# Even-layer bursts with the sums of values behind the scores, and odd-layer dilated scores on 64 rows with zero columns

## The chip, the cores and the metric

The kernel runs on one core of one Trainium2 chip. A core has a tensor engine (PE, whose weight loads are listed as PEld), a vector engine (DVE), a scalar engine (ACT), GpSimd (POOL) and queues that issue DMAs (here nearly all on SyncE, SP). The metric is the device time of one execution in microseconds (us), as the median of several runs. The profile is that of one execution.

## The reference

Two layers of a hybrid encoder trunk on one sequence of 256 tokens of width 1024, all in float32. Layer 0 is even, layer 1 is odd. Cut to what matters here:

```python
for layer in range(2):
    xn = rms_norm(x, norm_mix[layer])
    x = x + (even_mixer if layer % 2 == 0 else odd_mixer)(xn, ...)
    x = x + sq_relu_mlp(rms_norm(x, norm_mlp[layer]), w1[layer], w2[layer])
return rms_norm(x, norm_final)

# even: 8 heads of neighbourhood attention (scores + bias, softmax, sum of values) and
#       8 heads of latent attention (a 64-wide and a turned 32-wide part), side by side,
#       then one output projection of width 1024
# odd:  16 heads; for each of 3 groups of keys (window, stride) = (128,1), (512,4), (2048,16)
#       scores are taken at those offsets alone; the three groups are joined in one softmax:
sc = einsum('bqhd,bqjhd->bhqj', q_blk, k_sel) * scale     # per group, masked where outside
out = softmax over the three groups' entries, times their values, summed; then @ w_o
```

With 256 tokens, group 1 pairs each token with those of the same remainder modulo 4, and group 2 with those of the same remainder modulo 16. The kernel's host code orders the tokens so that the 64 tokens of one remainder modulo 4, a "class", stand together; a tile of 128 tokens then holds two classes, and the scores of groups 1 and 2 are needed only inside a class, a 64 by 64 block. A mask does the rest.

## The kernel before, in words

Everything lives on chip but the weights, which stream in as 64 or so chunks of 1 MB by DMA on SP's queue into four buffers `raw`. Products in float32 are made of parts that the tensor engine takes at full rate: each operand is split into a high part (a cast on ACT, L178) and a low part (a subtraction on DVE, L179), and a product is three matmuls (`mm3`, L182 to L184) or two (`mm2`, L188 and L189). Each weight chunk is so split in four pieces: four ACT casts `whi` and four DVE subtractions `wlo`. These pieces are spread over the whole program and share the two engines with the softmaxes. Some small matmuls (transposes, sums of values, and the odd layer's group 1 and 2 scores) take plain float32 instead.

The phases follow each other: even mixer, MLP 0, odd mixer, MLP 1 with the final norm. A tile framework schedules the instructions of each engine from the order in which the code issues them, from priorities (`soon()` raises that of the copies and splits that empty PSUM) and from its own estimates; a semaphore wait keeps each dependency. PSUM has eight banks here: four under the tag `acc` and four under `w`, and each tag is handed round in turn, so that a new tile waits until the tile that had the bank four allocations earlier has been read.

**Even mixer.** `main` is a list of 32 steps of large products: 12 steps of query and key projection (`qk_steps`, 12 mm3 matmuls of 256 columns each), 8 steps of latent queries, keys and values (12, 6 or 3 matmuls), and 12 steps of output projection (`out_steps`, 12 matmuls each; step 20 is the first). Behind some of the steps stands a `burst(hp)`: it handles one pair of heads (`hp` 0 to 3 neighbourhood, 4 to 7 latent):

- `turn_pair(hp - 1)` transposes the probabilities of the pair before (16 transposes, L748, into two `w` banks, copied out at L752 by ACT or DVE as `pts`);
- `pair_scores` or `latent_scores` makes the scores of pair `hp` (12 matmuls at L203 or 24 at L701, into two `w` banks). Their two heads j = 0 and 1 use rows 0 to 63 and 64 to 127 of the array. The softmax follows on DVE and ACT: maxima (L731 or L705), exponentials (L734 or L708), reciprocals, then the scaling to `pp` (L736 and L737, or L713 and L715), which the transposes of the next burst read;
- `mix(a, b)` makes the sums of values of two pairs, 32 matmuls at L767 (two instructions each) into one bank, `acc` as long as the output projection's four accumulators `accs` aren't open (step 19), `w` after; it reads the `pts` of both pairs and is split to `oa` or `ob`, which the output projection reads.

In a burst with a `mix`, the `mix` comes first, ahead of the transposes and scores. After step 31 and `mix(6, 7)` follow the last products (`out_last`, which need both splits of that `mix`), then `hand_over`, which prepares the MLP's input `xT`.

**Odd mixer.** Eight units of two heads. A unit's projections run as large products (`qk_steps`, `value_steps`); after the sixth step of unit u + 1 stands the `burst` of unit u: transposes of the unit before (L936, 12), scores of group 0 (`two_heads`, L203, 12), 12 more transposes, and the scores of groups 1 and 2 (L914): 16 matmuls, each of a class's 64 queries by its 64 keys, two instructions each, for i (tile of tokens), g (group), c (class in the tile) and j (head). Queries of both groups are in `q12`, keys in `k12`, both written by one DVE addition after the rotary turn (L890).

**Final norm.** The last 128 rows are scaled in two column parts, 640 by DVE and 384 by ACT, and each part leaves in one DMA, the first on SP's queue, the second on ACT's (L473 to L476).

Of the kernel before, what the change touches and what calls it, by code (L numbers as in the profile page):

```python
# [16 lines left out]
F32 = mybir.dt.float32  # L17
F32R = mybir.dt.float32r
AF = mybir.ActivationFunctionType
ALU = mybir.AluOpType  # L20
# [3 lines left out]
P = 128  # L24
D = 1024
KT = D // P
T = 256
NT = T // P
# [18 lines left out]
def trunk(ctx, tc, a, out):  # L47
    nc = tc.nc
# [26 lines left out]
    def halves(z):  # L75

        return (z[:, 0, :], z[:, 1, :]) if len(z.shape) == 3 else (z[:, :, 0, :], z[:, :, 1, :])

    def bank(tag):
        return ps.tile([P, 512], F32, tag=tag, name=tag)  # L80
# [96 lines left out]
    def split(hi, lo, src, eng=None):  # L177
        a = nc.scalar.copy(hi, src).ins  # L178
        return a, (eng or nc.vector).tensor_tensor(lo, src, hi.bitcast(F32), op=ALU.subtract).ins  # L179
# [38 lines left out]
    def tok(t):  # L218
        return slice(t * P, (t + 1) * P)
# [41 lines left out]
    def inverse_columns(s):  # L261

        inv = columns(s)
        nc.vector.reciprocal(inv, inv)
        return inv
# [148 lines left out]
    def finish(mp, xT, s):  # L414

        HALF = [slice(0, 512), slice(512, D)]
        g = mp.tile([P, D], F32, name="gain")
        nc.sync.dma_start(g, a["norm_final"].partition_broadcast(P))
        xt = mp.tile([P, NT, D], F32, name="xt")
        tail = range(13, 16)  # L420

        def tokens_first(j):

            if j % 2 == 0 and j < 8:
                t, h = j // 4, j // 2 % 2
                pt = bank("w")
                for k in range(4):
                    nc.tensor.transpose(pt[:, k * P:(k + 1) * P], x[:, 4 * h + k, tok(t)], ident)
                nc.scalar.copy(xt[:, t, HALF[h]], pt)

        accs, hs, inv, w = mlp(mp, xT, lambda: inverse_columns(s), tail, make_down([15] * 3 + [tail[0] - 1]), tokens_first)
        jf = [(j, f) for j in w for f in range(2)]
        for j, f in jf:
            for h in range(2):
                mm_tokens(accs[h], hs, j, w[j], f, 0, h * 512, h * 512 + 512, False, (j, f) == (15, 1))

        def residual(t, cs, acc):
            nc.vector.scalar_tensor_tensor(xt[:, t, cs], acc, column(inv, t), xt[:, t, cs], ALU.mult, ALU.add)

        def square_sum(v, o):  # L440
            nc.scalar.activation(scratch([v.shape[-1]], "junk"), v, AF.Square, scale=D ** -0.5, accum_out=o)

        ss = work.tile([P, 4], F32, tag="ssf", name="ss")
        for h, cs in enumerate(HALF):
            residual(0, cs, accs[h])
            square_sum(xt[:, 0, cs], ss[:, h:h + 1])
        nc.vector.tensor_scalar(ss[:, 2:3], ss[:, 0:1], ss[:, 1:2], EPS, ALU.add, ALU.add)
        r = rsqrt(ss[:, 2:3], "x")
        for h, cs in enumerate(HALF):
            y = scratch([512], "y")  # L450
            nc.vector.scalar_tensor_tensor(y, xt[:, 0, cs], r, g[:, cs], ALU.mult, ALU.mult)
            nc.sync.dma_start(out[0:P, cs], y)


        ss = work.tile([P, 4], F32, tag="ssf", name="ss")
        xg = mp.tile([P, D], F32, name="xg")
        residual(1, HALF[1], accs[3])
        for i, (c0, c1) in enumerate(((0, 512), (512, 768), (768, D))):
            acc = bank("w") if i else accs[2]
            for n, (j, f) in enumerate(jf):  # L460
                mm_tokens(acc[:, 0:c1 - c0], hs, j, w[j], f, 1, c0, c1, i > 0 and n == 0, n == len(jf) - 1)
            v = xt[:, 1, c0:c1]
            residual(1, slice(c0, c1), acc[:, 0:c1 - c0])
            if i < 2:
                square_sum(v, ss[:, i:i + 1])
            else:
                nc.vector.tensor_scalar(ss[:, 2:3], ss[:, 0:1], ss[:, 1:2], EPS, ALU.add, ALU.add)
                nc.vector.tensor_tensor_reduce(out=scratch([c1 - c0], "junk"), in0=v, in1=v, op0=ALU.mult, op1=ALU.add,
                                               scale=1.0 / D, scalar=ss[:, 2:3], accum_out=ss[:, 3:4])
            nc.vector.tensor_tensor(xg[:, c0:c1], v, g[:, c0:c1], op=ALU.mult)  # L470
        r = rsqrt(ss[:, 3:4], "x")
        cs = slice(0, 640), slice(640, D)
        nc.vector.tensor_scalar(xg[:, cs[0]], xg[:, cs[0]], r, None, ALU.mult)  # L473
        nc.sync.dma_start(out[P:T, cs[0]], xg[:, cs[0]])
        nc.scalar.activation(xg[:, cs[1]], xg[:, cs[1]], AF.Copy, scale=r)
        nc.scalar.dma_start(out[P:T, cs[1]], xg[:, cs[1]])  # L476


    def even(ep):
# [291 lines left out]
                split(*halves(mixed[kind][:, hp:hp + n]), pvo[:, 0:n * T].rearrange("p (i n) -> p i n", i=n))  # L771

        def burst(hp, *mixes):
            if mixes:
                mix(*mixes)
            if hp > 0:
                turn_pair(hp - 1)
            if hp < 8:
                (pair_scores if hp < 4 else latent_scores)(hp)

        ug, kg = query_steps(), key_value_steps()
        first = qk_steps(0)
# [12 lines left out]
        main = [f for c in range(1, 4) for f in qk_steps(c)] + [kg[0], ug[0], ug[1], kg[1], kg[2], ug[2], kg[3], ug[3]]  # L795
        main += [f for k in range(6) for f in out_steps(accs, mixed, wo, k)]
        beside = {0: [turn_c[1]], 3: [turn_keys], 19: [lambda: accs.extend(open_accs())]}
        for at, *n in ((1, 0), (5, 1), (9, 2), (13, 3, 0, 1), (17, 4), (20, 5, 2, 3), (23, 6), (26, 7, 4, 5), (29, 8)):
            beside.setdefault(at, []).append(lambda n=n: burst(*n))
        beside.setdefault(31, []).append(lambda: mix(6, 7))  # L800
        for i, step in enumerate(main):
            step()
            run_all(beside.get(i, ()))
# [3 lines left out]
    def odd(op, xT, s):  # L807
# [5 lines left out]
            nc.sync.dma_start(dst, a[nm])  # L813
        mixed = [quarter_pair("oa"), quarter_pair("ob")]

        def unit_tiles(u):
            d = {}
            for n, shape, dt in (("q0", [P, 2, 2, T], F32R), ("q12", [P, 2, T], F32), ("k12", [P, 2, T], F32)):
                d[n] = op.tile(shape, dt, tag=n, name=n, bufs=2)
            return d  # L820

        values = {}
# [36 lines left out]
        def qk_steps(d):  # L859


            hold = {}

            def gemm(b, f, half):
                if f == 0 and half == 0:
                    hold["w"], hold["s"] = weight(), scratch([2, T], "qk")
                if half == 0:
                    hold["p"] = bank("acc")
                (wh, wl), s, pq = hold["w"], hold["s"], hold["p"]
                for k in range(4 * half, 4 * half + 4):  # L870
                    ws = slice((f * KT + k) * P, (f * KT + k + 1) * P)
                    mm2(pq, wh[:, ws], wl[:, ws], xT[:, k], k == 0, k == KT - 1)
                if half == 1:
                    with soon():
                        joined(s[:, f], pq)
                if f == 1 and half == 1:
                    rope(b, s)

            def rope(b, s):
                sw, r1 = scratch([2, T], "sw"), scratch([2, T], "r1")  # L880
                for r in range(0, P, 64):
                    nc.sync.dma_start(sw[r:r + 32], s[r + 32:r + 64])
                    nc.sync.dma_start(sw[r + 32:r + 64], s[r:r + 32])
                nc.vector.tensor_tensor(r1, s, cosT.unsqueeze(1).broadcast_to([P, 2, T]), op=ALU.mult)
                nc.vector.tensor_tensor(sw, sw, sinT.unsqueeze(1).broadcast_to([P, 2, T]), op=ALU.mult)
                if b == 0:
                    nc.vector.tensor_tensor(r1, r1, sw, op=ALU.add)
                    split(*halves(d["q0"]), r1)
                else:
                    nc.vector.tensor_tensor(d[("q12", "k12")[b - 1]], r1, sw, op=ALU.add)  # L890

            return [lambda v=(b, f, h): gemm(*v) for b in range(3) for f in range(2) for h in range(2)]

# [9 lines left out]
        def scores(u, d, between):  # L903

            ss = {(i, j): bank("w") for i in range(NT) for j in range(2)}
# [3 lines left out]
            for i in range(NT):  # L909
                for g in range(2):  # L910
                    for c in range(2):
                        for j in range(2):
                            pb, own = slice(64 * j, 64 * j + 64), slice(i * P + 64 * c, i * P + 64 * c + 64)
                            nc.tensor.matmul(ss[i, j][64 * c:64 * c + 64, T + 64 * g:T + 64 * g + 64], d["q12"][pb, g, own],  # L914
                                             d["k12"][pb, g, own], start=True, stop=True)
            for i in range(NT):
                for j in range(2):
                    sn, pp = scratch([384], "sn"), op.tile([P, 384], F32, tag="pp", name="pp", bufs=4)
                    mn, z, rz = (work.tile([P, 1], F32, tag=v, name=v, bufs=4) for v in ("dmn", "dz", "drz"))
# [44 lines left out]
        d = units[0]  # L964
# [154 lines left out]
```

## Time and profile before

| | |
|---|---|
| median of 3 runs | 736.02 us (735.62 to 736.18) |
| the profiled execution | 735.57 us, of which the span from first to last instruction is 733.8 us |
| mean granted clock of the tensor engine | 0.998 |
| DVE, ACT, POOL busy | 536.9 us (73%), 452.4 us (62%), 5.7 us (1%) |
| DMA | 135.72 MB, mean 185 GB/s |

A view by time lists start and duration of an instruction (or of a run of like ones, with their count) and, in brackets, how long its engine stood idle before it and whose end ended that. Matmuls overlap, and their ends are modelled, so the pace of the tensor engine is read from the distance of two starts, and not from the durations. A row "64\*128" says how many rows and columns of the array an instruction takes.

### The profile page before, as it was taken

How to read it: one execution, taken by the hardware profiler on the slowest of the kernel's cores; microseconds unless marked ns; L12 is line 12 of the kernel's file. 1: busy time of each engine (PE TensorE's matmuls, PEld its weight loads, DVE VectorE, ACT ScalarE, POOL GpSimd, SP SyncE). 2: the span in 40 equal slices, each digit the busy share in tenths (PEclk: the TensorE clock that was granted, in tenths of full speed). 3: DMA queues.
4: the chain of work that ended last, by engine and by line, in shares of the span. 5: the costliest groups of instructions: out<-in, count | busy, mean ns of one | idle time of the engine just before them, and what ended most of it. 6: DMA issues, size and time to landing. Idle time of an engine off the chain costs nothing.

```text
span 733.8 us, 12891 instructions
## 1 busy us (share of the span) xinstructions
PE 723.0 (99%) x5004; PEld 626.1 (85%) x5004; DVE 536.9 (73%) x1078; ACT 452.4 (62%) x1002; POOL 5.7 (1%) x16
## 2 busy tenths in 40 slices
PE   8999999999999999999999999999999999999996
PEld 5899989888888888888888888888998888888885
DVE  6799859756656656889778889778759666665664
ACT  7687857445445446856777667767857445544541
POOL 0100000000000000000000000000000000000000
PEclk9999999999999999999999999999999999999999
DMA  8864423565565554566755665466345556456501
GB/s 288 340 226 153 146 96 125 210 209 180 186 206 182 186 204 158 198 215 209 245 167 178 205 202 202 154 221 200 130 169 206 196 175 225 174 172 209 181 14 57
DMA packets 26989, 135.72 MB, mean 185 GB/s; under 512 B 4400, under 2 KB 7216, under 8 KB 12336
## 3 DMA queue, kind: packets, MB, share of 16 engines
q1 hardware_dynamic: 26640, 134.69, 53.2%
q8 instruction: 39, 0.64, 0.3%
q10 hardware_dynamic: 288, 0.21, 0.1%
q14 instruction: 22, 0.18, 0.1%
HBM read 127.55 MB, written 1.05 MB: 175 GB/s over the span
## 4 chain that ended last, share of the span: by engine, by line
PE 86%; DVE 4%; DMA 3%; ACT 3%; issue 2%; SPq 1%; POOL 0%; POOLq 0%
PE w L188 16%; PE acc L182 13%; PE acc L183 13%; PE acc L184 13%; PE acc L188 12%; PE w L189 8%; PE acc L189 6%; DVE wlo L179 2%; DMA raw<-in_w_c 1%; DMA raw<-in_w_qk 1%; ACT pp L734 1%; DMA bias<-in_rpb 1%; PE w L203 1%; PE acc L936 1%; PE acc L953 1%
## 5 line engine op out<-in xcount | busy, mean ns | idle before, releaser
L179 DVE TENSOR_TENSOR wlo<-raw,whi 128x512 fp32r<-128x512 f32 (+2 forms) x472 | 301.9, 681 | 70.5 <-ACT whi L178 68.8
L178 ACT CAST whi<-raw 128x512 fp32r<-128x512 f32 (+2 forms) x472 | 262.8, 617 | 86.1 <-issue 70.4
L188 PE MATMUL w<-xT,whi 128*128 128x512 f32 x512 | 178.2, 393 | 0.0
L188 PE MATMUL acc<-xT,whi 128*128 128x512 f32 x384 | 133.1, 395 | 0.0
L189 PE MATMUL w<-xT,wlo 128*128 128x256 f32 x512 | 132.8, 280 | 0.0
L188 PEld LDWEIGHTS w<-xT,whi 128*128 128x128 f32 x512 | 93.6, 188 | 17.3
L189 PEld LDWEIGHTS w<-xT,wlo 128*128 128x128 f32 x512 | 96.4, 188 | 5.3
L189 PE MATMUL acc<-xT,wlo 128*128 128x256 f32 x384 | 99.6, 280 | 0.0
L182 PE MATMUL acc<-whi,h 128*128 128x512 f32 x250 | 98.1, 392 | 0.0
L183 PE MATMUL acc<-wlo,h 128*128 128x512 f32 x250 | 97.5, 390 | 0.0
L184 PE MATMUL acc<-whi,h 128*128 128x512 f32 x250 | 97.4, 390 | 0.0
L188 PEld LDWEIGHTS acc<-xT,whi 128*128 128x128 f32 x384 | 69.6, 188 | 12.8
L195 ACT COPY up<-w 128x256 f32<-128x256 f32 x64 | 23.9, 373 | 87.3 <-PE w L188 87.2
L189 PEld LDWEIGHTS acc<-xT,wlo 128*128 128x128 f32 x384 | 72.2, 188 | 3.7
L196 DVE TENSOR_TENSOR up<-up,w 128x256 f32<-128x256 f32 x64 | 26.8, 419 | 61.4 <-ACT up L195 61.4
L184 PEld LDWEIGHTS acc<-whi,h 128*128 128x128 f32 x250 | 46.9, 188 | 9.8
L183 PEld LDWEIGHTS acc<-wlo,h 128*128 128x128 f32 x250 | 47.0, 188 | 9.6
L182 PEld LDWEIGHTS acc<-whi,h 128*128 128x128 f32 x250 | 47.0, 188 | 8.8
L183 PE MATMUL acc<-wlo,xT 128*128 128x512 f32 (+1 forms) x128 | 50.4, 394 | 0.8 <-DVE wlo L179 0.8
L182 PE MATMUL acc<-whi,xT 128*128 128x512 f32 (+1 forms) x128 | 50.5, 394 | 0.5 <-ACT whi L178 0.5
L184 PE MATMUL acc<-whi,xT 128*128 128x512 f32 (+1 forms) x128 | 50.0, 391 | 0.0
L855 ACT ACTIVATE v<-acc,rstd 64x128 f32<-64x128 f32 x64 | 22.8, 362 | 19.7 <-PE acc L184 14.0
(203 smaller groups left out, 981.7 us busy)
## 6 DMA issues: line engine op xcount, KB each, us to landing
raw<-in_w SPq DMA_DIRECT2D x64, 1024.0 KB, 4.8
raw<-in_w_oqk SPq DMA_DIRECT2D x24, 1024.0 KB, 5.0
raw<-in_w_ov SPq DMA_DIRECT2D x12, 1024.0 KB, 5.3
sw<-qk SPq DMA_DIRECT2D x96, 64.0 KB, 3.1
raw<-in_w_qk SPq DMA_DIRECT2D x4, 1024.0 KB, 11.1
raw<-in_w_oe SPq DMA_DIRECT2D x4, 1024.0 KB, 5.0
raw<-in_w_oo SPq DMA_DIRECT2D x4, 1024.0 KB, 5.9
bias<-in_rpb SPq DMA_DIRECT2D x8, 256.0 KB, 4.3
```

Of the source, the lines that this page charges most:

```text
L178: a = nc.scalar.copy(hi, src).ins
L179: return a, (eng or nc.vector).tensor_tensor(lo, src, hi.bitcast(F32), op=ALU.subtract).ins
L182: nc.tensor.matmul(o, sh, mh, start=first, stop=False)
L183: nc.tensor.matmul(o, sh, ml, start=False, stop=False)
L184: nc.tensor.matmul(o, sl, mh, start=False, stop=last)
L188: both = lambda: nc.tensor.matmul(o, sh, m.rearrange("p v n -> p (v n)"), start=first, stop=last)
L189: low = lambda: nc.tensor.matmul(o[:, 0:T], sl, m[:, 0, :], start=False, stop=False)
L195: nc.scalar.copy(dst, o[:, T:2 * T])
L196: nc.vector.tensor_tensor(dst, dst, o[:, 0:T], op=ALU.add)
L203: nc.tensor.matmul(o[j], qk[pb, 0, a, ts], qk[pb, 1, b, :], start=n == 0, stop=n == 2)
L734: nc.scalar.activation(pp[:, j], sn[:, j], AF.Exp, bias=mn[:, j:j + 1], scale=-1.0, accum_out=z[:, j:j + 1])
L855: nc.scalar.activation(v12[64 * g - 64:64 * g, 2 * i + c, :], pq[rows, cs], AF.Copy, scale=ri[rows])
```

## The change

Three edits.

1. In the even mixer, a `burst` now issues transposes and scores first and its `mix` last, and the table of bursts is new: `mix(0, 1)` moves from step 13 to step 9, `mix(2, 3)` from 20 to 17, `mix(4, 5)` from 26 to 22; bursts 6, 7 and 8 come one step earlier (22, 25, 28), and `mix(6, 7)` at step 30, so that step 31 stands between it and the last products.
2. In the odd mixer, `q12` becomes one of two fixed tiles `spread` with a third slot of 64 zeros between the two classes of each group and token tile. The matmul of class c takes 128 columns of it: class 0 with the zeros behind, or the zeros with class 1 behind. So both classes' matmuls write all 128 output rows, the second one adding to the first. There are as many instructions as before, on 64 rows and 128 columns of the array instead of 64 and 64. POOL writes the zeros once, in two memsets; DVE writes the queries around them.
3. In the final norm, the last rows are cut at 512 and 512 columns instead of 640 and 384.

```diff
-        cs = slice(0, 640), slice(640, D)
+        cs = HALF
...
         def burst(hp, *mixes):
-            if mixes:
-                mix(*mixes)
             if hp > 0:
                 turn_pair(hp - 1)
             if hp < 8:
                 (pair_scores if hp < 4 else latent_scores)(hp)
+            if mixes:
+                mix(*mixes)
...
-        for at, *n in ((1, 0), (5, 1), (9, 2), (13, 3, 0, 1), (17, 4), (20, 5, 2, 3), (23, 6), (26, 7, 4, 5), (29, 8)):
+        for at, *n in ((1, 0), (5, 1), (9, 2, 0, 1), (13, 3), (17, 4, 2, 3), (20, 5), (22, 6, 4, 5), (25, 7), (28, 8)):
             beside.setdefault(at, []).append(lambda n=n: burst(*n))
-        beside.setdefault(31, []).append(lambda: mix(6, 7))
+        beside.setdefault(30, []).append(lambda: mix(6, 7))
...
+        spread = [op.tile([P, 2 * NT, 3, 64], F32, name=f"spread{i}") for i in range(2)]
+        for z in spread:
+            nc.gpsimd.memset(z[:, :, 1, :], 0.0)
...
-            for n, shape, dt in (("q0", [P, 2, 2, T], F32R), ("q12", [P, 2, T], F32), ("k12", [P, 2, T], F32)):
+            for n, shape, dt in (("q0", [P, 2, 2, T], F32R), ("k12", [P, 2, T], F32)):
                 d[n] = op.tile(shape, dt, tag=n, name=n, bufs=2)
+            d["q12"] = spread[u % 2]
...
+                elif b == 1:
+                    own = lambda z: z.rearrange("p g (t c n) -> p (g t) c n", t=NT, c=2)
+                    nc.vector.tensor_tensor(d["q12"][:, :, 0:3:2, :], own(r1), own(sw), op=ALU.add)
                 else:
-                    nc.vector.tensor_tensor(d[("q12", "k12")[b - 1]], r1, sw, op=ALU.add)
+                    nc.vector.tensor_tensor(d["k12"], r1, sw, op=ALU.add)
...
-                            nc.tensor.matmul(ss[i, j][64 * c:64 * c + 64, T + 64 * g:T + 64 * g + 64], d["q12"][pb, g, own],
-                                             d["k12"][pb, g, own], start=True, stop=True)
+                            nc.tensor.matmul(ss[i, j][:, T + 64 * g:T + 64 * g + 64], d["q12"][pb, 2 * g + i, c:c + 2, :],
+                                             d["k12"][pb, g, own], start=c == 0, stop=c == 1)
```

Three places of the scheduled order, on the two engines that wait for each other in the even mixer.

On PE, burst 6 of the even mixer before: the transposes of pair 5 (L748), then the scores of pair 6 (L701), which are listed in twos, one for each head.

```order
L184 MATMUL acc<-oa,wlo 128x256
L748 MATMUL w<-ident,pp 128x64 x16
L701 MATMUL w<-mk,mq 128x256 x2
L701 MATMUL w<-kT,mq 128x256 x2
L701 MATMUL w<-mk,mq 128x256 x2
```

The same burst now:

```order
L184 MATMUL acc<-oa,wlo 128x256
L748 MATMUL w<-ident,pp 128x64 x4
L701 MATMUL w<-mk,mq 128x256 x2
L701 MATMUL w<-kT,mq 128x256 x2
L748 MATMUL w<-ident,pp 128x64 x12
L701 MATMUL w<-mk,mq 128x256 x2
```

Four of the scores now stand between the first four transposes and the other twelve. Ahead of this burst stand 24 output products (two steps) since burst 5, where there were 36; behind it now comes `mix(4, 5)`.

On DVE, between the softmax of pair 4 and that of pair 5, before: `oa` is the low split of `mix(2, 3)`, `mq` that of a latent query, L705 are the maxima of pair 5's scores.

```order
L709 RECIPROCAL rz<-z 128x2
L179 TENSOR_TENSOR wlo<-raw,whi 128x512 x2
L179 TENSOR_TENSOR mq<-qm,mq 128x2x256
L179 TENSOR_TENSOR wlo<-raw,whi 128x512 x2
L179 TENSOR_TENSOR oa<-w,oa 128x2x256
L179 TENSOR_TENSOR wlo<-raw,whi 128x512 x3
L705 TENSOR_REDUCE mn<-w 128x2 x2
L179 TENSOR_TENSOR wlo<-raw,whi 128x512
```

The same stretch now:

```order
L674 COPY vml<-acc 128x512
L179 TENSOR_TENSOR oa<-acc,oa 128x2x256
L649 TENSOR_TENSOR qm<-acc,turns 128x512
L179 TENSOR_TENSOR wlo<-raw,whi 128x512 x2
L179 TENSOR_TENSOR mq<-qm,mq 128x2x256
L179 TENSOR_TENSOR wlo<-raw,whi 128x512 x5
L705 TENSOR_REDUCE mn<-w 128x2 x2
L179 TENSOR_TENSOR wlo<-raw,whi 128x512
```

The split `oa` has moved up, ahead of the weight pieces; the maxima still stand behind seven weight pieces and ahead of the eighth.

On DVE, at the end of the even mixer before: `pts` is the copy of pair 7's transposes, `ob` the low split of `mix(6, 7)`, L304 the first residual addition.

```order
L179 TENSOR_TENSOR wlo<-raw,whi 128x512 x3
L752 COPY pts<-w 128x512
L179 TENSOR_TENSOR wlo<-raw,whi 128x512 x5
L179 TENSOR_TENSOR ob<-w,ob 128x2x256
L304 TENSOR_TENSOR x<-acc,x 128x512
```

The same place now:

```order
L752 COPY pts<-w 128x512
L179 TENSOR_TENSOR wlo<-raw,whi 128x512 x2
L179 TENSOR_TENSOR ob<-w,ob 128x2x256
L179 TENSOR_TENSOR wlo<-raw,whi 128x512 x2
L304 TENSOR_TENSOR x<-acc,x 128x512
```

Two weight pieces instead of five stand between the copy and the split, and two have moved behind the split. In the odd mixer PE's order is the same as before, instruction by instruction, with the new form of the scores in the old places.

## The prediction

> **What bounds the kernel now.** I read the page first (busy shares, chain), then busy time by stretches, then the tensor engine (PE) by time around each burst, and last the queues of DVE and ACT where PE stood.
>
> ```profile
> PE 723.0 (99%) x5004; PEld 626.1 (85%) x5004; DVE 536.9 (73%) x1078; ACT 452.4 (62%) x1002; POOL 5.7 (1%) x16
> PE 86%; DVE 4%; DMA 3%; ACT 3%; issue 2%; SPq 1%; POOL 0%; POOLq 0%
> 36.00:114.00 78.00, 75.81 (x930) 71.23 (x930) 63.14 (x155) 57.64 (x152) 0.00 (x0) 1.00 0.45 158
> 305.00:536.00 231.00, 231.00 (x1857) 200.51 (x1857) 189.65 (x405) 167.12 (x386) 0.33 (x1) 1.00 0.60 199
> ```
>
> PE is the bound. In the odd mixer (305 to 536 us) it never stands, so an instruction that PE takes longer over is paid in full. In the even mixer (36 to 114 us) it is idle for 78.00 - 75.81 = 2.2 us. More than that is lost there, which shows if bursts are compared, here burst 5 with burst 6:
>
> ```profile
> 76.45 0.71 PE L748 MATMUL w<-ident,pp 64*128 64x64 f32 x16
> 76.97 0.36 PE L701 MATMUL w<-mk,mq 64*128 64x256 f32 x1
> 78.90 0.38 PE L701 MATMUL w<-mk,mq 64*128 64x256 f32 x1 [0.86 <-ACT pts L752]
> 80.52 0.39 PE L182 MATMUL acc<-oa,whi 128*128 128x256 f32 x1
> ...
> 84.99 0.71 PE L748 MATMUL w<-ident,pp 64*128 64x64 f32 x16
> 85.51 0.36 PE L701 MATMUL w<-mk,mq 64*128 64x256 f32 x2
> 87.11 0.39 PE L182 MATMUL acc<-oa,whi 128*128 128x256 f32 x1
> ```
>
> From the first transpose to the first product behind, burst 6 takes 87.11 - 84.99 = 2.12 us, burst 5 takes 80.52 - 76.45 = 4.07 us. A sum of values ahead of burst 5 has taken a fifth bank of the four `w`, so the second head's scores wait for a copy, and the first head's go alone (x1, not x2: half the rows idle, yet counted as busy).
>
> **The even mixer, gains.** Now the sums stand behind the scores and the first two of them in `acc` banks: transposes and scores find four free `w` banks, and burst 5 should take 2.12 us. That is **-1.95 us**. Burst 7 has the same fault, and the end another:
>
> ```profile
> 93.60 0.71 PE L748 MATMUL w<-ident,pp 64*128 64x64 f32 x16
> 94.12 0.36 PE L701 MATMUL w<-mk,mq 64*128 64x256 f32 x1
> 95.08 0.39 PE L701 MATMUL w<-mk,mq 64*128 64x256 f32 x2 [0.24 <-DVE ob L179]
> 96.69 0.39 PE L182 MATMUL acc<-oa,whi 128*128 128x256 f32 x1
> ...
> 91.58 2.08 PE L767 MATMUL w<-pts,vml 128*64 128x64 f32 x64
> 104.81 2.08 PE L767 MATMUL w<-pts,vml 128*64 128x64 f32 x64
> 107.58 0.73 PE L182 MATMUL acc<-ob,whi 128*128 128x256 f32 x4 [0.69 <-ACT ob L178]
> 108.61 0.39 PE L183 MATMUL acc<-ob,whi 128*128 128x256 f32 x1 [0.29 <-DVE ob L179]
> ```
>
> Burst 7: 96.69 - 93.60 = 3.09 us against 2.12, **-0.97 us**. The end: sums take 93.60 - 91.58 = 2.02 us to the next instruction, so the last products could start at 106.83; they start at 107.58 (0.75 late), and four of them take 1.03 us instead of about 0.5, since the low part comes after five weight pieces on DVE. Now a step of 12 products stands between (36 products took 91.58 - 87.11 = 4.47 us, so 12 take 1.49), and the split has no weight piece of its time ahead of it. The split's low part was ready some 1.2 us after 106.83 even behind weight pieces (its product went at 108.61 instead of about 107.4); the step of 1.49 covers that. **-1.2 us**.
>
> **The even mixer, the new wait.** Burst 5 was late on PE, but was its softmax waiting for it?
>
> ```profile
> 70.82 0.60 DVE pts L752
> 71.42 0.61 DVE mn L705
> ...
> 72.05 0.47 ACT L708 ACTIVATE pp<-w,mn 128x256 f32<-128x256 f32 x1 [1.71 <-DVE mn L705]
> 79.21 1.69 ACT L178 CAST whi<-raw 128x512 fp32r<-128x512 f32 x3
> 81.10 1.28 DVE L705 TENSOR_REDUCE mn<-w 128x2 f32<-128x512 f32 x2
> 83.99 0.91 ACT L715 ACTIVATE pp<-pp,rz 128x256 f32<-128x256 f32 x2 [0.23 <-DVE rz L709]
> ```
>
> It was not. ACT runs from 72.05 to the three casts at 79.21 with no idle time, DVE's low parts follow, and the maxima of pair 5 start at 81.10 behind seven of them. In the new order the same 18 ACT instructions stand between the two softmaxes, and DVE's maxima again behind seven weight pieces. The stretch starts earlier only by the DVE copy `pts` at 70.82 (0.60 us; both copies are ACT's now). Of that I take 0.35, since `mix(0, 1)` pushes the inputs of pair 3 back by some 2 us and DVE slips by an estimated 0.25 there. So pair 5's probabilities come not at 83.99 + 0.91 = 84.90 but at 84.55. PE is sooner: burst 5 starts near 76.45 again (the same work stands ahead), ends at 78.57, and 24 products instead of 36 (4.47 x 24/36 = 2.98) bring it to burst 6 at 81.55. It waits inside the transposes until 84.55; then 4 transposes and 20 of the 24 scores remain, 0.13 + (87.11 - 85.51) x 20/24 = 1.46, to 86.0. Without a wait it would be 81.55 + 2.12 = 83.67. **+2.35 us**: burst 5's gain is taken back one burst later. Behind PE's waiting transposes stand scores, `mix(4, 5)` and all products; nothing else on PE can go ahead.
>
> Bounds of this wait: none, if ACT and DVE reach pair 5's maxima when PE delivers them (78.6 + 3.8 from 81.10 to 84.90 = 82.4, leaving 0.3); 3.5, if they slip by two more pieces of 0.6 us. I take 2.35, the value of the queues' own rows.
>
> Smaller ones. `mix(0, 1)` now follows burst 2's scores directly:
>
> ```profile
> 53.99 0.96 PE L203 MATMUL w<-qk 64*128 64x256 f32 x12
> 54.88 0.38 PE L182 MATMUL acc<-xT,whi 128*128 128x256 f32 x1
> 55.76 0.68 DVE L752 COPY pts<-w 128x512 f32<-128x512 f32 x1
> 68.95 0.39 PE L701 MATMUL w<-kT,mq 64*128 64x256 f32 x2
> 69.62 0.60 DVE mk L179
> ```
>
> The sums would start at 54.88, and after pair 0's half and a quarter of pair 1's (some 1.2 us) they need the copy that DVE ends at 55.76 + 0.68 = 56.44: about 0.4 us of waiting. PE gets it back at burst 4, where the scores wait anyway for the latent query that DVE finishes at 69.62. I put the two together at 0 (0 to +0.4). Even mixer: -1.95 - 0.97 - 1.2 + 2.35 = **-1.8 us** (-3.9 to -0.4).
>
> **The odd mixer.** One unit on PE:
>
> ```profile
> 359.50 0.59 PE L936 MATMUL acc<-ident,pp 64*128 64x64 f32 x12
> 359.90 0.96 PE L203 MATMUL w<-q 64*128 64x256 f32 x12
> 360.70 0.53 PE L936 MATMUL acc<-ident,pp 64*128 64x64 f32 x12
> 361.16 0.69 PE L914 MATMUL w<-k,q 64*64 64x64 f32 x32
> 361.78 0.50 PE L188 MATMUL acc<-xT,whi 128*128 128x512 f32 x1
> ```
>
> The 32 instructions of L914 take 361.78 - 361.16 = 0.62 us, way out included: four quarters of the array (two heads by two classes) work at once. With 128 columns each, only the two row halves can: 16 pairs. The price of a pair with 64 moving columns is that of the sums, 64 in 2.02 us or 0.063 us a pair, and of the transposes L748 (64 rows, 128 columns, the new form's own shape), 16 in 85.51 - 84.99 = 0.52 us or 0.065. So 16 x 0.063 = 1.01 us, plus some 0.03 since the way out is spread there over twice as many: +0.42. What is saved is the change of shape on the way in: 12 transposes take 361.16 - 360.70 = 0.46 us ahead of L914 and 359.90 - 359.50 = 0.40 ahead of L203, of the same shape as they; I take 0.09 (0.06 to 0.12, as the first twelve pay a way in themselves). Net +0.33 a unit, eight units: **+2.6 us** (2.2 to 2.9), all on PE's path. Softmaxes start 0.3 us later, with the products of a whole unit until the next burst as cover.
>
> The Trainium skill, "TensorEngine Tiling (Array Packing)", section Key Properties, says that a change of tiling mode drains the engine. The two twelves agree, at 0.06 us. By that rule alone, with the matmuls at their old pace, the sum would lose 8 x 0.12 = 1.0 us here instead of gaining 2.6; this is a rival below.
>
> At nothing: the two memsets (POOL is 5.7 us busy in all, and its next instruction comes a phase of products later), and DVE's addition into a tile with gaps (the same 512 elements; 0.1 us more on an engine that waits on nothing's path there). If DVE were short, 8 x 0.1.
>
> **The end.**
>
> ```profile
> 729.43 0.62 ACT L475 ACTIVATE xg<-xg,rstd 128x384 f32<-128x384 f32 x1 [2.91 <-POOL rstd L225]
> L317 ACT ACTIVATE down<-acc,ms 128x512 f32<-128x512 f32 x4 | 2.7, 674 | 0.5 <-PE acc L184 0.5
> out<-xg SPq DMA_DIRECT2D x1, 320.0 KB, 2.4
> out<-xg ACTq DMA_DIRECT2D x1, 192.0 KB, 2.7
> ```
>
> ACT's half ends last, in issue and in landing (2.7 us against 2.4). With 512 columns the scaling takes 0.67 (L317) instead of 0.62, and its DMA carries 256 KB, though both together carry as much as before: between 0 and +0.3, I take **+0.1 us**.
>
> **The sum.** -1.8 + 2.6 + 0.1 = +0.9 us. The profiled execution took 735.57 us (733.8 of span and 1.8 around it), so 736.5 on its footing; the median shown is 736.02, 0.45 above it, so **736.9 us**.
>
> **Rivals.**
> 1. The wait at burst 6 hardly comes (0.3 instead of 2.35), because DVE and ACT have the maxima when PE delivers. Against it stands the order, with seven weight pieces ahead. -1.1 in all: 734.9 us. Chance 0.10.
> 2. Slower by more: one mechanism, at burst 3. Pair 3's queries come 2 us later than now; if DVE finishes their low part after PE reaches burst 3's scores (near 63 us), each weight piece of 0.6 us queued ahead delays the whole stretch to burst 6. It decides from two pieces: 2 x 0.6 = +1.2, so 738.1 us. For it speaks that I count a margin of only some 0.2 us in DVE's queue there (an estimate); against it that the early `oa` split goes into time in which DVE stands. Chance 0.22.
> 3. The drain is what the scores cost, and 64 by 128 goes at the pace of 64 by 64: -1.8 - 1.0 + 0.1 = -2.7, so 733.3 us. Two instructions on the same columns would have to overlap, which no row shows. Chance 0.05.
> 4. Row halves don't overlap in the accumulating form: 16 x 0.063 more in each unit, +8 us, 745 us. The sums accumulate at full pace. Chance 0.03.
>
> My forecast has 0.60. A measurement of this kernel can tell about 0.2%, 1.5 us, from no change. The forecast (735.9 to 737.8) is within that in nine parts of ten, rival 1 too; 2, 4 and the forecast's upper edge are slower; 3 is faster. That makes faster 0.06, same 0.62, slower 0.32. The range takes in rivals 1 and 2: 734.8 to 738.4.
>
> **What would show it.** In the changed kernel: L701 in twos from burst 5 on, and burst 5 near 2.1 us; a gap of over 2 us inside L748 of burst 6, put down to L713 or L715; no wait of the last products for `ob`; the new scores' 32 instructions at about 1.05 us; first product of MLP 0 1.8 us sooner. The forecast is wrong if burst 6 shows no gap, if the scores' row shows 0.6 us, or if new gaps stand before 64 us.

## The result, and the profile after

The changed kernel takes 744.12 us (median of 4 runs, 743.30 to 745.49) against 736.0 us before: a ratio of 1.0111, with a 95% interval from 1.0099 to 1.0123. It is slower by 8.1 us, outside the range on record.

Two views carry the reading. First the busy time by stretches of the changed kernel: even mixer and odd mixer, each as a length, then busy time and count of PE, PEld, DVE, ACT and POOL, and the granted clock.

```profile
36.00:114.00 78.00, 75.81 (x943) 71.52 (x942) 64.24 (x156) 59.83 (x156) 0.01 (x1) 1.00 0.41 145
305.00:545.00 240.00, 239.47 (x1852) 209.40 (x1853) 190.00 (x400) 167.18 (x385) 0.00 (x0) 1.00 0.57 189
```

The second stretch was taken 9 us longer than the 305 to 536 us of before and holds about as many instructions of PE (1852 against 1857); PE is idle in 0.53 us of it. So almost all of the loss is not a wait: PE takes longer over the same number of instructions. The view by time, on PE, of the first product of each MLP, before:

```profile
113.88 0.39 PE L188 MATMUL w<-xT,whi 128*128 128x512 f32 x1
548.62 0.39 PE L188 MATMUL w<-xT,whi 128*128 128x512 f32 x1
```

and in the changed kernel:

```profile
112.65 0.39 PE L188 MATMUL w<-xT,whi 128*128 128x512 f32 x1
557.47 0.39 PE L188 MATMUL w<-xT,whi 128*128 128x512 f32 x1
```

| stretch | before to after |
|---|---|
| up to MLP 0's first product | -1.23 us |
| from there to MLP 1's first product (MLP 0, and the odd mixer) | (557.47 - 112.65) - (548.62 - 113.88) = +10.08 us |
| from there to the end of the span | (742.5 - 557.47) - (733.8 - 548.62) = -0.15 us |

The first row holds some start-up scatter. The transposes of burst 1, ahead of all that the change touches, begin at 46.40 us instead of 45.98, 0.43 late; the granted clock stood at 0.60 and 0.55 from 8 to 12 us in this execution and at 1.00 in that of before. Taken from burst 1, the even mixer is 1.65 us shorter.

Where the 10 us come from shows in one odd unit of the changed kernel, on PE by time:

```profile
360.76 0.53 PE L944 MATMUL acc<-ident,pp 64*128 64x64 f32 x12
361.13 1.95 PE L922 MATMUL w<-k,spread 64*128 64x64 f32 x32
363.01 0.50 PE L188 MATMUL acc<-xT,whi 128*128 128x512 f32 x1
```

The 32 instructions of the new scores (L922) take 363.01 - 361.13 = 1.88 us where L914 took 0.62. The way in is shorter, as forecast: 361.13 - 360.76 = 0.37 us instead of 0.46. A unit so costs 363.01 - 360.76 = 2.25 us instead of 361.78 - 360.70 = 1.08, **+1.17 us**, 9.4 in eight units. The rest is one new wait, in unit 3 (the first unit is 0): twelve transposes (L944) start 0.81 us after the last score ahead of them where 0.12 is usual, 0.7 us lost, 0.53 of it listed as idle. All waits that the profile lists on PE in the changed kernel (waited for, us, times, longest):

```profile
PE w L748 <- DVE pp L713: 1.4, 1, 1.4
PE acc L92 <- DVE warm L86: 1.2, 1, 1.2
PE acc L182 <- ACT whi L178: 1.1, 1, 1.1
PE acc L944 <- DVE qk L196: 0.5, 1, 0.5
PE w L748 <- DVE pp L736: 0.3, 1, 0.3
PE w L748 <- ACT pp L715: 0.2, 1, 0.2
PE acc L767 <- DVE pts L752: 0.2, 1, 0.2
PE acc L183 <- DVE wlo L179: 0.2, 1, 0.2
```

Those of L92, L182 and L183 lie ahead of burst 1; the kernel before has 1.2, 0.5 and 0.8 us there. And the even mixer's bursts 5 and 6 in the changed kernel, on PE by time:

```profile
77.33 0.71 PE L748 MATMUL w<-ident,pp 64*128 64x64 f32 x16
77.86 0.36 PE L701 MATMUL w<-mk,mq 64*128 64x256 f32 x2
...
79.46 0.38 PE L182 MATMUL acc<-oa,whi 128*128 128x256 f32 x1
...
82.26 0.28 PE L184 MATMUL acc<-oa,wlo 128*128 128x256 f32 x1
83.94 0.34 PE L748 MATMUL w<-ident,pp 64*128 64x64 f32 x4 [1.41 <-DVE pp L713]
84.06 0.48 PE L701 MATMUL w<-mk,mq 64*128 64x256 f32 x2
84.26 0.40 PE L701 MATMUL w<-kT,mq 64*128 64x256 f32 x2
84.90 0.74 PE L748 MATMUL w<-ident,pp 64*128 64x64 f32 x12 [0.24 <-ACT pp L715]
...
86.81 2.08 PE L767 MATMUL w<-pts,vml 128*64 128x64 f32 x64
```

Burst 5 takes 79.46 - 77.33 = 2.13 us (4.07 before). Burst 6 ends 86.81 - 82.26 = 4.55 us after the last product ahead of it; burst 5's own way in (0.21) and 2.12 would make 2.33. So 2.2 us are waited inside burst 6, of which the profile lists 1.41 + 0.24 = 1.65 us as idle.

### The profile page after: what moved, and what is told of

Its sections match the earlier page's. It is cut to its first block, busy times and chain, and to the rows that moved or that the text cites. A ratio compares the mean times of both kernels' runs of the same rounds, so it can differ in the third digit from the quotient of the medians.

```text
span 742.5 us, 12889 instructions
## 1 busy us (share of the span) xinstructions
PE 731.2 (98%) x5004; PEld 636.5 (86%) x5004; DVE 538.4 (73%) x1076; ACT 454.3 (61%) x1004; POOL 6.2 (1%) x18
## 3 DMA queue, kind: packets, MB, share of 16 engines
HBM read 127.55 MB, written 1.05 MB: 173 GB/s over the span
## 4 chain that ended last, share of the span: by engine, by line
PE 87%; DVE 4%; ACT 4%; DMA 2%; issue 2%; SPq 1%; POOL 0%; POOLq 0%; DVEq 0%; ACTq 0%
PE w L188 16%; PE acc L182 14%; PE acc L183 13%; PE acc L184 13%; PE acc L188 10%; PE w L189 8%; PE acc L189 5%; DVE wlo L179 2%; PE w L922 2%; DMA sw<-qk 2%; ACT pp L734 1%; PE acc L944 1%; DMA raw<-in_w_c 1%; PE w L203 1%; PE w L701 1%
## 5 line engine op out<-in xcount | busy, mean ns | idle before, releaser
L182 PE MATMUL acc<-whi,h 128*128 128x512 f32 x250 | 98.1, 392 | 0.0
L183 PE MATMUL acc<-wlo,h 128*128 128x512 f32 x250 | 97.5, 390 | 0.0
L183 PEld LDWEIGHTS acc<-wlo,h 128*128 128x128 f32 x250 | 46.9, 188 | 9.6
L182 PEld LDWEIGHTS acc<-whi,h 128*128 128x128 f32 x250 | 47.0, 188 | 8.7
L182 PE MATMUL acc<-whi,xT 128*128 128x512 f32 (+1 forms) x128 | 51.2, 400 | 1.1 <-ACT whi L178 1.1
L183 PE MATMUL acc<-wlo,xT 128*128 128x512 f32 (+1 forms) x128 | 50.6, 395 | 0.2 <-DVE wlo L179 0.2
```

Of the source, the lines that this page charges most:

```text
L182: nc.tensor.matmul(o, sh, mh, start=first, stop=False)
L183: nc.tensor.matmul(o, sh, ml, start=False, stop=False)
```

## The experiments

Open at this point: why do 16 pairs of 64-row matmuls take 1.88 us, and not the 1.05 of the forecast? Three theories. **Weight columns**: an instruction of the new form holds 128 columns of weights (the queries with their zeros) where L914 held 64, and loading them sets the pace. **Moving columns or quarters**: it is the work streamed through, or any sharing of columns, that costs. **Adding**: two instructions that add into the same outputs hinder each other. The view of single sources speaks for the first. Weight loads (PEld) of the old scores, of the sums and of the transposes, before (shortest/median/longest in ns, first and last start, rows by columns of the array):

```profile
L914 PEld LDWEIGHTS w<-k,q x256: 129/135/135, 330.8 to 515.9; 64*64 64x64 f32 x128
L767 PEld LDWEIGHTS w<-pts,vml x128: 133/138/138, 91.6 to 106.6; 128*64 128x64 f32 x128
L748 PEld LDWEIGHTS w<-ident,pp x128: 134/139/142, 46.0 to 101.6; 64*128 64x128 f32 x128
L701 PEld LDWEIGHTS w<-mk,mq x48: 182/185/194, 68.6 to 96.2; 64*128 64x128 f32 x48
```

and of the new scores, in the changed kernel:

```profile
L922 PEld LDWEIGHTS w<-k,spread x256: 183/188/195, 329.5 to 524.8; 64*128 64x128 f32 x128
```

The new scores load like L701, which has 128 columns of weights too, and not like the sums (64 columns) or the transposes (128 columns, but a transpose), from which the forecast took its price.

### The odd edit alone

The changed kernel with bursts, their table and the final norm as before:

```diff
-        cs = HALF
+        cs = slice(0, 640), slice(640, D)
...
         def burst(hp, *mixes):
+            if mixes:
+                mix(*mixes)
...
-            if mixes:
-                mix(*mixes)
...
-        for at, *n in ((1, 0), (5, 1), (9, 2, 0, 1), (13, 3), (17, 4, 2, 3), (20, 5), (22, 6, 4, 5), (25, 7), (28, 8)):
+        for at, *n in ((1, 0), (5, 1), (9, 2), (13, 3, 0, 1), (17, 4), (20, 5, 2, 3), (23, 6), (26, 7, 4, 5), (29, 8)):
```

> The odd edit alone; bursts and final norm as before. If the odd scores are the whole loss (32 instructions in 1.88 us instead of 0.62, less 0.09 on the way in, eight units: 9.4 us), 745.4 us against 736.0, with a pace of 0.112 us a pair in each unit. If part of the loss came from the even edit's shifted schedule, less: my own sum on record would give +2.6, 738.6 us.

745.82 us (745.46 to 747.49, 4 runs) against 735.98 in the same runs: 1.0139 (1.0123 to 1.0154), +9.8 us. The scores take 1.88 us a unit here too, and unit 3 has the wait of L944 again (0.27 us listed as idle). The odd edit is the whole loss, and it costs almost four times the +2.6 on record.

### Twice the moving columns

Every pair streams the keys of both classes, 128 columns instead of 64:

```diff
-                            nc.tensor.matmul(ss[i, j][:, T + 64 * g:T + 64 * g + 64], d["q12"][pb, 2 * g + i, c:c + 2, :],
-                                             d["k12"][pb, g, own], start=c == 0, stop=c == 1)
+                            nc.tensor.matmul(ss[i, j][:, T + 128 * g:T + 128 * g + 128], d["q12"][pb, 2 * g + i, c:c + 2, :],
+                                             d["k12"][pb, g, i * P:i * P + P], start=c == 0, stop=c == 1)
```

> The changed kernel, with 128 keys (both classes) instead of 64 streamed past each pair of odd scores; group 2's columns land where the softmax doesn't read them, so the output is not the reference's. If loading 128 float32 weight columns sets the pace, 128 moving columns hide behind it: 0.112 us a pair as with 64, 32 instructions in 1.88 us, and the same time as the changed kernel, 744 us. If the pace is that of the moving columns at half speed (or of row halves that don't overlap), a pair takes 0.22, a unit 3.6 us, +14 us: 758.

One run: 746.25 us. One unit on PE by time in this kernel:

```profile
361.36 0.54 PE L944 MATMUL acc<-ident,pp 64*128 64x64 f32 x12
361.73 2.01 PE L922 MATMUL w<-k,spread 64*128 64x128 f32 x32
363.66 0.50 PE L188 MATMUL acc<-xT,whi 128*128 128x512 f32 x1
```

363.66 - 361.73 = 1.93 us against 1.88, with twice as much streamed. The moving side doesn't set the pace. (The program is some 2 us longer than the changed kernel all the same: the even mixer of this execution lost another 1.5 us, which is taken up below, and a second unit waits at L944, 0.60 us.)

### No adding

Class 1's pair writes columns of its own, and every matmul starts and ends its sum:

```diff
-                            nc.tensor.matmul(ss[i, j][:, T + 64 * g:T + 64 * g + 64], d["q12"][pb, 2 * g + i, c:c + 2, :],
-                                             d["k12"][pb, g, own], start=c == 0, stop=c == 1)
+                            nc.tensor.matmul(ss[i, j][:, T + 128 * c + 64 * g:T + 128 * c + 64 * g + 64], d["q12"][pb, 2 * g + i, c:c + 2, :],
+                                             d["k12"][pb, g, own], start=True, stop=True)
```

> The changed kernel, but the matmuls of class 1 write their own columns and add to nothing; the softmax doesn't read those, so class 1's odd scores of groups 1 and 2 are left out of the output. If 128 weight columns set the pace, still 0.112 us a pair and 744 us. If adding the second class onto the first costs the time, 0.06 us a pair, a unit 1.0 us, 8 x 0.8 = 6.5 us less: 737.5 us.

One run: 743.22 us. The same place in this kernel:

```profile
360.75 1.95 PE L922 MATMUL w<-k,spread 64*128 64x64 f32 x32
362.63 0.50 PE L188 MATMUL acc<-xT,whi 128*128 128x512 f32 x1
```

362.63 - 360.75 = 1.88 us, as with the adding. This execution has no wait at L944, and from MLP 0's first product (112.25 us) to MLP 1's (556.36) it takes 444.11 us, 9.37 more than the 434.74 of before: the 9.4 of the eight units alone. Rival 4 of the prediction, whose 745 us came nearest to the result, had named the adding: its time was near by luck, its cause is not what happens.

### The same columns, with 64 columns of weights

The old form, with the class loop outermost, so that eight pairs of matmuls follow each other on the same 64 columns before the other 64 get theirs:

```diff
-            for i in range(NT):
-                for g in range(2):
-                    for c in range(2):
+            for c in range(2):
+                for i in range(NT):
+                    for g in range(2):
                         for j in range(2):
```

> The kernel before with one change: the loop over the classes of the group 1 and 2 scores stands outermost, so that eight pairs of instructions follow each other on columns 0 to 63 and then eight on columns 64 to 127, each still 64 rows by 64 columns; nothing is left out and nothing added up. Pairs now share their columns, as in the changed kernel, but each instruction holds 64 columns of weights and not 128. If the number of weight columns sets a pair's pace: about 0.06 us a pair, the 32 instructions in 0.93 to 1.05 us with the way out (0.62 in the kernel before, 1.88 in the changed one), 3 us for eight units, 738.5 to 739.5. This is also what the prediction on record priced for the new form. If any pair that shares its columns goes at 0.11 us whatever its width: 1.8 us a unit, 745. If pairs on the same columns cost nothing over quarters: 0.62 us, 736.

One run: 739.78 us, beside 735.58 before. The same place in this kernel:

```profile
361.70 0.98 PE L914 MATMUL w<-k,q 64*64 64x64 f32 x32
362.61 0.50 PE L188 MATMUL acc<-xT,whi 128*128 128x512 f32 x1
```

362.61 - 361.70 = 0.91 us. Pairs that share 64 columns of weights follow each other at 0.058 us (starts in the trace: 51 ns to the next pair and 7 inside it), pairs that share 128 columns at 0.112 us (107 and 5). The forecast's 0.063 would have been right for this kernel; for the new form the width of the weights had to be counted. The time is 4.2 us longer and not 2.3 (8 x 0.29) because PE waits here too, twice ahead of L914 for the dilated keys of DVE (L890), 1.5 us in all, which no theory had foreseen:

```profile
PE w L914 <- DVE k L890: 1.5, 2, 1.2
```

The Trainium skill, "TensorE: Matmul & The Clock Gate", section "LDWEIGHTS (loading the stationary operand)", gives the load time as the number of columns over 1.2, in ns, whatever the number of rows: 107 ns for 128 columns, 53 for 64. The 112 and 58 ns a pair agree with it within about 5 ns; the transposes L748, 128 columns at 60 to 65 ns a pair, don't, so that a transpose is no row to take a matmul's price from. As the transposes write 128 output rows too, the number of rows written is not the price either.

### The even edit alone

The kernel before with the new `burst` and its table, old scores and old final norm (the even part of the diff of the change, word for word).

> The even edit alone; odd scores and final norm as before. By the steps on record (bursts 5 and 7 at 2.1 us, no wait at the end, a new wait of 2.35 us in burst 6) -1.8 us: 734.2 us. If the even edit has a share in the loss, 736 us or more.

735.38 us (733.85 to 736.12, 11 runs): 0.9985 (0.9976 to 0.9994). That is -0.6 us, against -1.8 on record and the 1.65 that the changed kernel's own trace shows. The profiled execution of this kernel explains the difference. From burst 1's transposes to MLP 0's first product:

| kernel | even mixer | us |
|---|---|---|
| before; odd edit alone; final norm alone; class by class | old | 67.90; 67.96; 67.96; 67.99 |
| the changed kernel; no adding | new | 66.25; 66.26 |
| even edit alone; twice the moving columns | new | 67.89; 67.76 |

The same code, in the same order, gives 66.25 or 67.8. What differs is the granted clock, whose changes the traces record. In the even edit alone it was full for 81.92 us, half from 86.11 to 89.52 us, and full again; with twice the moving columns it was full for 78.51 us and half from 84.48 to 87.89 us; in the kernel before it was full for 727.04 us without a break. These lengths are 24, 23 and 213 times 3.413 us, and the times at half are 3.41 us each. So each execution can be cut into stretches of 3.41 us with edges where its clock changed. Here are such stretches in the profiled execution of the even edit alone (length, busy time of PE, PEld, DVE, ACT and POOL, then the granted clock):

```profile
82.70:86.11 3.41, 2.08 (x34) 1.83 (x36) 1.90 (x6) 2.73 (x9) 0.00 (x0) 1.00 0.81 286
86.11:89.52 3.41, 3.41 (x58) 3.19 (x56) 1.99 (x6) 1.67 (x7) 0.00 (x0) 0.50 0.36 149
```

and in that of the changed kernel:

```profile
80.07:83.48 3.41, 2.47 (x22) 2.27 (x20) 3.37 (x8) 2.49 (x9) 0.00 (x0) 1.00 0.82 267
83.48:86.89 3.41, 2.70 (x42) 2.33 (x44) 1.44 (x4) 2.12 (x7) 0.00 (x0) 1.00 0.81 283
86.89:90.30 3.41, 3.41 (x76) 3.34 (x77) 2.45 (x7) 2.66 (x10) 0.00 (x0) 1.00 0.17 70
```

Both wait in burst 6. In the first one 3.41 - 2.08 = 1.33 us of idle time fall into one stretch, and the granted clock of the next is half, which loses 3.41 / 2 = 1.7 us. In the second one the wait lies across an edge (0.94 and 0.71 us idle), and the clock stays at 1.00. The other two executions with this even mixer fit: twice the moving columns has 1.66 us of idle time in one stretch (81.06 to 84.48) and the drop behind it, no adding has 0.49 and 1.12 us in two and no drop. So the wait can be paid a second time, by where it falls on these stretches, and 1.65 - 1.7 leaves nothing of the gain. In the ten profiled executions, from the first full clock to the final norm, 1.31 us or more of idle time in a stretch were followed by half the clock each time and 1.15 us or less were not, with one exception at 0.86 us, which comes below. Over all timed executions the mean granted clock is 0.996 or less in 7 of 11 of this kernel and in 2 of 21 of the kernel before, though that mean alone doesn't tell where the clock fell; the other four have a median of 734.47 us, 1.5 under the kernel before. The Trainium skill, "TensorE: Matmul & The Clock Gate", section "What's actually happening", says that the clock follows a free-running activity window of 3.4 us and is halved after an idle one. The length and the free run agree with the multiples above; but no stretch ahead of a drop was idle throughout, 1.33 us of 3.41 were enough.

### The final norm alone

The kernel before with `cs = HALF`.

> The final norm's cut alone. On record +0.1 us (0 to +0.3) since ACT's DMA gets more bytes: 736.1. The rival, that both DMAs share the same engines and only the sum of their bytes counts: -0.1 us, 735.9. Either is near what can be told.

735.86 us (735.07 to 736.93, 11 runs): 1.000 (0.9992 to 1.0009). No effect that can be measured.

### The end of the even mixer alone

The kernel before with only the last burst and the last sums earlier:

```diff
-        ..., (20, 5, 2, 3), (23, 6), (26, 7, 4, 5), (29, 8)):
+        ..., (20, 5, 2, 3), (23, 6), (26, 7, 4, 5), (28, 8)):
-        beside.setdefault(31, []).append(lambda: mix(6, 7))
+        beside.setdefault(30, []).append(lambda: mix(6, 7))
```

> The kernel before with the last two entries alone moved: burst 8 at step 28, mix(6, 7) at step 30, sums ahead of transposes as before. If the wait of the last products for the split of mix(6, 7) is what the end costs, -1.2 us: 734.8 us, with bursts 5 and 7 as long as before (4.1 and 3.1 us). If the order of the burst (sums last) is needed for it, 736 us.

734.85 us (734.30 to 736.44, 11 runs): 0.9986 (0.9977 to 0.9995), -1.0 us against -1.2 on record. No product waits for `ob` in its trace. Its profiled execution is one of its slowest (736.11 us): there the clock falls to half from 80.6 to 84.0 us, behind burst 5 in its old form, with its half-used scores and its wait. Less the 1.7 us of the drop, its 68.42 us from burst 1 to MLP 0 are 66.7, and 1.2 under the 67.90 of before. So such a drop isn't peculiar to the new wait. The stretch ahead of it has 0.86 us of idle time; with 0.84 to 0.86 at the same burst no drop followed in the kernel before, the odd edit alone, the final norm alone and class by class, and why it came here stays open.

### Sums behind the scores, with the bursts where they were

If the wait at burst 6 takes burst 5's gain back because only 24 products stand between the two, 36 should return most of it. The kernel before with the new order inside `burst` and this table, old scores and old final norm:

```diff
-        for at, *n in ((1, 0), (5, 1), (9, 2), (13, 3, 0, 1), (17, 4), (20, 5, 2, 3), (23, 6), (26, 7, 4, 5), (29, 8)):
+        for at, *n in ((1, 0), (5, 1), (9, 2, 0, 1), (13, 3), (17, 4, 2, 3), (20, 5), (23, 6, 4, 5), (26, 7), (29, 8)):
...
-        beside.setdefault(31, []).append(lambda: mix(6, 7))
+        beside.setdefault(30, []).append(lambda: mix(6, 7))
```

> As the even edit alone, but bursts 6, 7 and 8 at steps 23, 26 and 29, so that 36 products instead of 24 stand between bursts 5 and 6; mix(6, 7) at step 30. If burst 6 waits for the softmax of pair 5, whose time ACT and DVE set, its wait of 2.2 us shrinks by the 1.49 us of 12 products, and the program is some 1.4 us faster than the even edit alone: 732.8 us. If the wait came with the new place of the sums (banks, or the order on PE), it stays: 734.2 us.

**733.09 us** (732.49 to 733.28, 5 runs): 0.9959 (0.9947 to 0.9972). It is faster than both kernels. Burst 6 on PE by time in this kernel:

```profile
82.59 0.28 PE L184 MATMUL acc<-oa,wlo 128*128 128x256 f32 x1
82.86 0.34 PE L748 MATMUL w<-ident,pp 64*128 64x64 f32 x4
83.82 0.74 PE L748 MATMUL w<-ident,pp 64*128 64x64 f32 x12 [0.62 <-ACT pp L715]
...
86.05 2.08 PE L767 MATMUL w<-pts,vml 128*64 128x64 f32 x64
```

86.05 - 82.59 = 3.46 us instead of 4.55: half of the wait is gone, 1.09 us of the 1.49 that were expected. Counted from burst 1 (45.34 us here), the last twelve transposes start at 83.82 - 45.34 = 38.48 us, and in the changed kernel at 84.90 - 46.40 = 38.50. So ACT and DVE set that time, and PE only comes later to it; but no scores stand between the transposes here to fill the wait. The time is 2.3 us under that of the even edit alone and not 1.4, which fits the clock that most executions of that kernel lose. From burst 1 to MLP 0 it takes 65.20 us, 2.7 less than before and 1.05 less than the changed kernel; the granted clock is 0.998 or more in all five executions. That the shorter wait is what keeps the clock up fits, but five executions don't show it.

## Why the prediction was wrong

The step that failed is the price of the new scores: "The price of a pair with 64 moving columns is that of the sums, 64 in 2.02 us or 0.063 us a pair, and of the transposes L748 (64 rows, 128 columns, the new form's own shape), 16 in 85.51 - 84.99 = 0.52 us or 0.065." The kind of term was right (16 pairs instead of quarters, all on PE's path), its size was not: a pair takes 0.112 us, so the scores went from 0.62 to 1.88 us and not to 1.05. Both rows fitted the moving side only; the sums hold 64 columns of weights, and a transpose's load is short. A third row stood in a fence of the prediction itself: L701 in twos has 64 rows, 128 columns and is a true matmul, and its pairs stand 0.12 us apart (with 256 moving columns, so no more than an upper end). Taken as the far end, it gives 16 x 0.12 = 1.9 us a unit, and a bound of 8 x (1.92 - 0.62 - 0.09) = +9.7 us in place of +2.9.

- **Burst 5, -1.95; burst 7, -0.97.** Right: 2.13 and 2.12 us in the changed kernel.
- **The end, -1.2.** Right: no product waits for `ob`. From the end of the sums to MLP 0's first product it takes 7.15 us with a step of 12 products (1.4 us) more, where 113.88 - 106.83 = 7.05 were taken before, so -1.3; alone the edit brings -1.0.
- **The new wait in burst 6, +2.35.** Right in place, cause and size: 2.2 us, put down to L713 and L715. On the time of before (0.42 us earlier) the last twelve transposes start at 84.48 us, against 84.55 on record. Rival 1 is out.
- **Burst 2, 0 (0 to +0.4).** The wait came as forecast (from the sums to the product behind them 57.76 - 55.30 = 2.46 us instead of 2.02, +0.44), but it was not won back at burst 4, where the transposes now wait for L736. It is paid: counted from burst 1, burst 5 begins 0.46 us later than before, just over the +0.4 allowed.
- **Even sum, -1.8.** -1.65 where the clock stays up; the terms as measured (-1.94, -0.97, -1.3, +2.2, +0.46) add up to -1.55. The bounds of the terms on record add up to -3.8 and -0.2, not -3.9 and -0.4. That the wait could be followed by half the clock for 3.4 us was not considered, and it takes the gain away in some of the executions. Rival 2 (a slip at burst 3) didn't occur: nothing new waits there.
- **The way in, -0.09 a unit.** Right: 0.37 us instead of 0.46. Rival 3, scores at their old pace, is out.
- **The odd sum, +2.6.** Measured 9.4 by the units and 0.7 by the wait of unit 3 (L944 for DVE's `qk`), for which no term stood; alone +9.8.
- **At nothing.** DVE's addition into the tile with gaps takes 0.68 us, as it did without (L896 now, L890 before).
- **The final norm, +0.1.** No effect that can be measured.

On its own footing the corrected sum is -1.65 + 9.4 + 0.7 + 0 = +8.4 us; with 0.43 of start-up scatter +8.9, and the profiled executions differ by 744.32 - 735.57 = 8.75.

## What to carry to other kernels

Price a small matmul from rows that match it on the weight side (columns of weights, and matmul or transpose), not only on the moving side: filling up weights with zeros to make a larger tile is paid by the column. A gain that comes from an earlier burst is worth only what the softmax behind it allows, so keep the distance between bursts at least as long as that softmax's queue. And a wait of the tensor engine can be paid twice: behind two of four waits of the same kind the granted clock was halved for as long as 3.4 us.

## What the runs showed of the hardware

- Matmuls on opposite row halves overlap also when both write all 128 output rows, each into its own bank, and add to what stands there: the two of a pair start 1 to 5 ns apart in most pairs.
- A pair of 64-row float32 matmuls follows the next after 0.112 us with 128 columns of weights, with 64 or with 128 moving columns, and after 0.058 us with 64 and 64; transposes of 64 rows by 128 columns take 0.060 to 0.065 us a pair.
- In all ten profiled executions the changes of the granted clock lie whole multiples of 3.413 us apart. The same wait of 1.4 and 0.2 us on PE was followed by half the clock for 3.41 us where 1.33 and 1.66 us of idle time fell into one such stretch, and not where it was split into 0.94 and 0.71, or 0.49 and 1.12.
